# Loads of the next tile's input and of the last weight moved from ScalarE's DMA queue to GpSimd's, behind three small copies

## The chip, the cores and the metric

One core of one Trainium2 chip runs the whole kernel. The metric is the device time of one execution in microseconds; lower is better. Every run shown had the full TensorE clock granted.

## The reference, cut to what matters

One layer, 2048 tokens of width 1024, everything in float32. All weights below are inputs.

```
h = rms_norm(x) * g                                   # per token
u = h @ w_in   -> conv v, B, C, gate z | q, k, v, gate z | merge gate logits (2 x 1024)
y_a = (B * conv3(C * v) * silu(z)) @ w_conv_out        # causal depthwise, width 3
y_b = (window_attention(q, k, v, sinks) * silu(z_a)) @ w_attn_out   # window 128, 16 heads, 4 kv heads
g_a, g_b = sigmoid(gate logits + gate_b)
out = x + (g_a * y_a + g_b * y_b) @ w_out
```

## The kernel before

The 2048 tokens are two tiles of 1024. For each tile the program goes through the same stages: k, v and q projections, the four conv projections, the gates, the gated branches `za` and `z`, then `ya` (conv output projection) and at the end `yb` (attention output projection, which also adds the two gated branches). After both tiles the output projection `o` multiplies all tokens by `w_out`. Attention is woven into the projections and is over before `ya`.

TensorE (PE) works in banks of 128 x 512 results. Each float32 product is three passes in a reduced format, since every operand is kept as a high part, rounded by ScalarE (ACT), and a low part, the rest, subtracted by VectorE (DVE). Most stages use a seven-product scheme for 2 x 2 blocks, whose operands are sums of quarter blocks of the input; DVE forms these sums. The `yb` stage has plain products: four units, each of four banks, each bank 24 matmuls in two halves of 12. Two banks in PSUM alternate, so PE can begin a bank only when DVE has read the bank two before it.

The order on each engine is fixed by hand. A counter `tick` counts half banks; `put(n, f)` lays a step `f` at tick `n`, and `run` records PE's work with the steps due. Each engine then runs its own list in order and waits, at the head of the list, for what an instruction needs. A DMA is an instruction in the list of the engine that issues it. Its landing is counted on one of eight counters, taken in turn; DMAs of SyncE (SP) and ACT share one set of eight, GpSimd (POOL) has another eight. An issue also waits until the last DMA on its counter has landed.

During `yb` of a tile this happens beside PE:

- SP loads, for each pair of banks, two gate tiles `thb` (from `gd`) and two partial results `m` (from `md`); DVE reads a bank into `thb` (line 213, SCALAR_TENSOR_TENSOR `thb<-thb,yb`), adds `m`, and SP stores the result to `mt`. Two `thb` pairs exist, so a pair is loaded when the pair two before it has been stored.
- In tile 0, `next_tile` prepares tile 1: ACT issues eight loads of `x` (512 KB each, by tokens, `ld`), squares them (`xsq`, line 526) into row sums, DVE turns the sums into roots with a chain of 12 small steps per pair of `x` blocks and a copy into `rt` (line 530), PE transposes the roots (`ptr`, line 536), ACT copies them to `rb` (line 538). Two such sets exist: blocks 0 to 3 and 4 to 7. ACT also issues 16 loads of the transposed input, `h` (256 KB each, `raw_load`, line 561), DVE multiplies each by `rb` and the gain (`norm_l`, `norm_r`), and the sums and splits `oph` follow.
- In tile 1, `wo_side` loads `w_out` in 16 pieces `wo` of 256 KB, issued by ACT (line 1271), and forms its sums and splits. There are no squares and no roots in it.

GpSimd has work in the attention (moves, masks, stores) and none in `ya` and `yb`.

Of the kernel before, what the change touches and what calls it, by code (L numbers as in the profile page):

```python
# [8 lines left out]
F32 = mybir.dt.float32  # L9
# [6 lines left out]
P = 128  # L16
D = 1024
KC = D // P
T = 1024
H = 512  # L20
# [41 lines left out]
def block_kernel(  # L62
# [12 lines left out]
    nc = tc.nc  # L75
    S = x.shape[1]
    NT = S // T
    x2, out2, xt2, w_in2 = x[0], out[0], xt, w_in
    w_co, w_ao, w_o = w_conv_out, w_attn_out, w_out[0]
# [7 lines left out]
    small = ctx.enter_context(tc.tile_pool(name="small", bufs=12))  # L87
# [6 lines left out]
    def slot(shape, dt, name):  # L94
        return big.tile(shape, dt, tag="big", name=name)

    def optile(name, shape=(P, 2, H), dt=F32R):
        return oppool.tile(list(shape), dt, tag="op", name=name)
# [25 lines left out]
    def hs(q):  # L124
        return slice(q * H, (q + 1) * H)
# [117 lines left out]
    def add(o, a, b, eng=None):  # L243
        return (eng or vec).tensor_tensor(out=o, in0=a, in1=b, op=ALU.add)

    def sub(o, a, b, eng=None):
        return (eng or vec).tensor_tensor(out=o, in0=a, in1=b, op=ALU.subtract)
# [172 lines left out]
    def spare(name):  # L420
        return consts.tile([P, H], F32, tag="s5", bufs=2, name=name)
# [96 lines left out]
    def x_load(t, b, eng):  # L518
        xt = optile(f"x{t}_{b}", (P, D), F32)
        r0 = t * T + b * P  # L520
        eng.dma_start(xt, x2[r0 : r0 + P, :])
        return xt

    def x_square(xt, ss, i, junk=None):

        nc.scalar.activation(out=xt if junk is None else junk, in_=xt, func=AF.Square, accum_out=ss[:, i : i + 1])
# [31 lines left out]

    def raw_load(t, q, c, st):
        h = st["raw"][c, q] = slot([P, H], F32, f"h{t}_{q}_{c}")  # L560
        nc.scalar.dma_start(h, xt2[c * P : (c + 1) * P, t * T + q * H : t * T + (q + 1) * H])

    def norm_l(t, c, st):
        x_norm(st["raw"][c, 0], c, st["rb"][0])
# [6 lines left out]
    def norm_r(t, c, st):  # L571

        x_norm(st["raw"][c, 1], c, st["rb"][1])
# [11 lines left out]
    def last_sum(j, st, to=None):  # L585

        raw = st["raw"]
        o = st.setdefault("t4", {})[j] = raw[2 * j, 0] if to is None else to
        sub(o, raw[2 * j + 1, 0], raw[2 * j, 0])

    def form(t, m, j, st):
        raw = st["raw"]
        src = {8: (0, 1), 1: (0, 0), 2: (1, 0), 3: (1, 1), 5: (0, 0), 6: (0, 0), 7: (0, 1)}.get(m)
        op_split(t, m, j, raw[2 * j + src[0], src[1]] if src else st["t4"][j], st["ops"])
# [5 lines left out]
    def put(n, f):  # L600
        at.setdefault(max(n, tick[0] + 1), []).append(f)
# [537 lines left out]
    def split_op(src, name):  # L1139
        o = optile(name)  # L1140
        split(o[:, 0], o[:, 1], src)
        return o


    YB_CHUNKS = (0, 2, 4, 6, 1, 3, 5, 7)

# [16 lines left out]
    def quarters(order):  # L1163
        return [(hf, q) for q in order for hf in range(2)]

    def branch(t, key, j, opt, fin, order):
        u = unit((key, t, j))
        for n, (hf, q) in enumerate(quarters(order)):
            ps = bank(f"{key}{t}_{j}_{hf}_{q}")
            yield from mm_t(ps, u, hf, opt, q, n == 3)  # L1170
            fin(2 * j + hf, q, ps)
            yield
# [50 lines left out]
    def yb_unit(t, j, opt, order):  # L1223
        th, m1 = {}, {}

        def get(n):
            pair = upool.tile([P, 2 * H + 2], F32, tag="u", name=f"thb{t}_{j}_{n}")
            for i, (hf, q) in enumerate(quarters(order)[2 * n : 2 * n + 2]):
                k = 2 * j + hf
                th[k, q] = pair[:, hs(i)]  # L1230
                nc.sync.dma_start(th[k, q], gd[t][1][k, :, hs(q)])
                m1[k, q] = spare(f"m1{t}_{k}_{q}")
                nc.sync.dma_start(m1[k, q], md[t][k, :, hs(q)])

        def fin(k, q, ps):
            m = th[k, q]
            vec.scalar_tensor_tensor(
                out=m, in0=m, scalar=1.0, in1=ps, op0=ALU.add, op1=ALU.mult)
            add(m, m, m1[k, q])
            nc.sync.dma_start(mt[t][k, :, hs(q)], m)  # L1240

        return branch(t, "yb", j, opt, fin, order), get
# [22 lines left out]
    def wo_side(n0, st):  # L1265
        raw = st["raw"]

        def ld(c):
            for q in range(2):
                h = raw[c, q] = slot([P, H], F32, f"wo_{c}_{q}")  # L1270
                nc.scalar.dma_start(h, w_o[c * P : (c + 1) * P, hs(q)])

        def sums(j):
            a, b = 2 * j, 2 * j + 1
            sub(raw[a, 1], raw[b, 1], raw[a, 1])
            sub(raw[a, 0], raw[b, 1], raw[a, 0])

        for j in range(KP):
            for i in range(2):
                put(n0 + 2 * j + i, lambda c=2 * j + i: ld(c))  # L1280
            put(n0 + 6 + 2 * j, lambda j=j: form(2, 1, j, st))
            put(n0 + 7 + 2 * j, lambda j=j: sub(raw[2 * j, 0], raw[2 * j, 1], raw[2 * j, 0]))
            put(n0 + 8 + 2 * j, lambda j=j: form(2, 5, j, st))
            put(n0 + 9 + 2 * j, lambda j=j: sums(j))
            put(n0 + 17 + j, lambda j=j: form(2, 6, j, st))
            put(n0 + 28 + j, lambda j=j: form(2, 2, j, st))
            put(n0 + 30 + j, lambda j=j: form(2, 7, j, st))
            put(n0 + 22 + j, lambda j=j: last_sum(j, st))
            put(n0 + 32 + j // 2, lambda j=j: form(2, 3, j, st))
            put(n0 + 34 + j // 2, lambda j=j: form(2, 4, j, st))  # L1290
# [33 lines left out]
    for n in range(S // P // 2):  # L1324
        t, c0 = divmod(2 * n * P, T)
# [5 lines left out]
    def x_state(t):  # L1331
        return state.setdefault(t, {"raw": {}, "ops": {}, "x": {}, "ss": {}})
# [3 lines left out]
    st = x_state(0)  # L1336
    raw, ops, xs = st["raw"], st["ops"], st["x"]
# [26 lines left out]
    for n in range(KC // 2):  # L1364
        u, h = divmod(n, 2)
# [178 lines left out]
    def next_tile(t, n0):  # L1544

        st = x_state(t)
        raw, ops, xs = st["raw"], st["ops"], st["x"]

        def ld(b):
            xs[b] = x_load(t, b, nc.scalar)  # L1550

        def stats(b0):
            ss = st["ss"][b0] = small.tile([P, 2], F32, tag="sx", bufs=4, name=f"ss{t}_{b0}")
            junk = ps_s.tile([P, D], F32, tag="s", name=f"xsq{t}_{b0}")
            for i in range(2):
                x_square(xs[b0 + i], ss, i, junk)

        def norm(b0):
            q, i = divmod(b0, HB)
            if i == 0:  # L1560
                rt[q] = small.tile([P, HB], F32, tag="sr", bufs=2, name=f"rt{t}_{q}")
            seen_[b0] = x_rsqrt(t, b0, 2, st["ss"][b0], rt[q][:, i : i + 2])

        def roots(q):
            for b0 in (q * HB, q * HB + 2):
                seen_[b0]()
            st.setdefault("rb", {})[q] = x_roots(t, q, rt[q])

        rt, seen_ = {}, {}
        for b, n in enumerate((0, 1, 1, 2, 3, 4, 5, 6)):  # L1570
            put(n0 + n, lambda b=b: ld(b))
        for g, n in enumerate((4, 4, 8, 9)):
            put(n0 + n, lambda g=g: stats(2 * g))
        for g, n in enumerate((5, 6, 10, 11)):
            put(n0 + n, lambda g=g: norm(2 * g))
            put(n0 + n + 1, lambda g=g: seen_[2 * g]())
        for q, n in enumerate((8, 15)):
            put(n0 + n, lambda q=q: roots(q))
        for c in range(KC):
            put(n0 + 6 + c // 2, lambda c=c: raw_load(t, 0, c, st))  # L1580
            put(n0 + 8 + c // 2, lambda c=c: norm_l(t, c, st))
            put(n0 + (13 if c % 2 == 0 else 18) + c // 2, lambda c=c: raw_load(t, 1, c, st))
        for j in range(KP):
            put(n0 + 15 + j, lambda j=j: form(t, 1, j, st))
            put(n0 + 15 + j, lambda j=j: norm_r(t, 2 * j, st))
            put(n0 + 16 + j, lambda j=j: first_sum(j, st))
            put(n0 + 18 + j, lambda j=j: form(t, 5, j, st))
            put(n0 + 20 + j, lambda j=j: norm_r(t, 2 * j + 1, st))
            put(n0 + 21 + j, lambda j=j: third(2 * j + 1, st))
            put(n0 + 21 + j, lambda j=j: second_sum(j, st))  # L1590
            put(n0 + 24 + j, lambda j=j: form(t, 6, j, st))
            put(n0 + 28 + j, lambda j=j: form(t, 2, j, st))
            put(n0 + 30 + j, lambda j=j: form(t, 7, j, st))
            put(n0 + 25 + j, lambda j=j: last_sum(j, st))
            put(n0 + 32 + j // 2, lambda j=j: form(t, 3, j, st))
            put(n0 + 34 + j // 2, lambda j=j: form(t, 4, j, st))

    tick0 = 0
    for t in range(NT):
# [57 lines left out]
        n0 = tick[0]  # L1657
# [78 lines left out]
```

## Time and profile before

| | us |
|---|---|
| median of 3 runs | 1933.35 (1933.23 to 1933.41) |
| profiled execution, device time | 1935.05 |
| its span in the trace | 1933.3 |
| PE busy | 1914.6 (99%) |
| DVE busy | 1531.3 (79%) |
| ACT busy | 970.6 (50%) |
| POOL busy | 561.2 (29%) |

The trace counts its times from the start of the span. A timeline row gives start, duration, engine, line, operation and tiles (written `<-` read); in square brackets stands how long the engine was idle before it and what ended that. Engine names with a q (ACTq, SPq) are the queue of an engine: DMA issues stand there and are not counted as busy. Line 213 is a helper through which nearly all DVE work goes, line 240 the one of ACT's rounding copies; these are told apart by their tiles. `yb` of tile 0 lies at 808 to 900 us, `yb` of tile 1 at 1690 to 1777 us. The queues in the DMA part of the profile: q1 is SP's, q10 ACT's, q0 GpSimd's.

### The profile page before, as it was taken

Reading aid. Unit: us, or ns where it says so; the run is one execution under the profiler, and the core shown is the slowest. Engines: PE = TensorE matmul, PEld = TensorE weight load, DVE = VectorE, ACT = ScalarE, POOL = GpSimd, SP = SyncE. Lnnn points to the kernel's source line nnn. Section 1 sums busy time; section 2 is a strip of 40 time slices with the busy share of each in tenths; the row PEclk is TensorE's granted clock in tenths of the full one; section 3 lists DMA queues with packets and bytes.
Section 4 is the critical chain, followed back from the end, with each engine's and each line's share of the span. In section 5 each row is a group of like instructions: output and inputs, shape, how many; then the busy total and the mean of one; then the engine's idle time right before and its main releaser. Section 6 shows DMA issues by size and latency. Waiting matters only on the chain.

```text
span 1933.3 us, 27463 instructions
## 1 busy us (share of the span) xinstructions
PE 1914.6 (99%) x8774; PEld 1587.9 (82%) x8774; DVE 1531.3 (79%) x2612; ACT 970.6 (50%) x1932; POOL 561.2 (29%) x786
## 2 busy tenths in 40 slices
PE   9999999999999999999999999999999999999999
PEld 7778888888888888878878888888888888888887
DVE  7989899888886669679689788888998568766654
ACT  7655455556674344434555545556666335423221
POOL 2371443455663000000462433445554000000000
PEclk9999999999999999999999999999999999999999
DMA  8485454577776423884585554567776523776453
GB/s 305 104 218 170 152 169 158 179 219 233 230 239 214 149 102 131 299 295 156 149 222 144 171 158 140 167 210 247 235 239 210 194 99 125 254 262 191 157 173 111
DMA packets 219424, 366.55 MB, mean 190 GB/s; under 512 B 29264, under 2 KB 104016, under 8 KB 219280
## 3 DMA queue, kind: packets, MB, share of 16 engines
q1 hardware_dynamic: 189696, 288.96, 46.5%
q0 software_dynamic: 23680, 63.21, 12.0%
q10 hardware_dynamic: 5904, 12.62, 2.0%
q8 instruction: 70, 1.15, 0.2%
q14 instruction: 74, 0.61, 0.1%
HBM read 251.17 MB, written 113.51 MB: 189 GB/s over the span
## 4 chain that ended last, share of the span: by engine, by line
PE 84%; DVE 8%; DMA 4%; issue 2%; ACT 1%; POOL 1%; SPq 0%; DVEq 0%; ACTq 0%; POOLq 0%
PE Y L412 31%; PE yb L1155 5%; PE Vcv L412 5%; PE Xcv L412 4%; PE Xgb L412 2%; PE Vgb L412 2%; PE Xza L412 2%; PE Vza L412 2%; PE Vga L412 2%; PE Vo L412 2%; PE Xo L412 2%; PE Vz L412 2%; PE Xz L412 2%; PE po L1017 2%; PE Xga L412 2%; PE Vb L412 2%
## 5 line engine op out<-in xcount | busy, mean ns | idle before, releaser
L979 POOL DMA_DIRECT2D x<-fd x256 | 140.4, 554 | 87.9 <-DMA fd<-f 49.9
L1000 POOL TENSOR_SCALAR_AFFINE_SELECT xh<-xh 64x512 fp32r<-64x512 f32 x64 | 73.5, 1148 | 142.3 <-DVE xl L213 120.6
L952 ACT ACTIVATE p<-s,st,rq 128x128 f32<-128x128 f32 x256 | 113.2, 450 | 0.3 <-DMA od<-o 0.3
L972 POOL DMA_DIRECT2D fd<-f x64 | 36.8, 575 | 248.7 <-DVE f L213 217.0
L856 POOL DMA_DIRECT2D vd<-v x16 | 9.9, 624 | 335.3 <-DVE k_r L236 328.9
L1155 PE MATMUL yb<-opb,wyb_0h 128*128 128x512 f32 x256 | 79.3, 391 | 2.4 <-DVE thb L213 2.4
L412 PE MATMUL Xcv<-oph,wcv_ah 128*128 128x512 f32 x256 | 79.5, 392 | 0.0
L1155 PE MATMUL yb<-opb,wyb_1h 128*128 128x512 f32 x256 | 78.9, 389 | 0.0
L1000 POOL TENSOR_SCALAR_AFFINE_SELECT xl<-xl 64x512 fp32r<-64x512 f32 x64 | 69.3, 1083 | 4.4
L1155 PEld LDWEIGHTS yb<-opb,wyb_0h 128*128 128x128 f32 x256 | 47.6, 188 | 13.8 <-DVE thb L213 3.6
L1000 POOL TENSOR_SCALAR_AFFINE_SELECT yp<-yp 64x512 fp32r<-64x512 f32 x64 | 56.4, 882 | 4.2
L308 ACT CAST wcv_sh<-wcv_raw 128x1024 fp32r<-128x1024 f32 x16 | 16.9, 1057 | 79.1 <-DVE wcv_raw L213 79.1
L1155 PEld LDWEIGHTS yb<-opb,wyb_1h 128*128 128x128 f32 x256 | 48.0, 188 | 10.0
L213 DVE TENSOR_TENSOR o<-po,o 64x256 f32<-64x256 f32 x128 | 53.5, 418 | 2.7 <-ACT o L1029 1.6
L1000 POOL TENSOR_SCALAR_AFFINE_SELECT yp<-xl 64x512 fp32r<-64x512 f32 x64 | 54.5, 852 | 3.1
L412 PEld LDWEIGHTS Xcv<-oph,wcv_ah 128*128 128x128 f32 x256 | 47.3, 188 | 9.5
L774 POOL DMA_DIRECT2D q2d<-q_h x64 | 44.3, 692 | 26.7 <-ACT q_h L769 21.5
L213 DVE TENSOR_TENSOR ophc<-zin,ophc 128x512 fp32r<-128x512 f32 x64 | 42.4, 688 | 10.8 <-ACT ophc L240 10.8
L213 DVE SCALAR_TENSOR_TENSOR y<-u,cols,y 128x512 f32<-128x512 f32 x64 | 49.2, 770 | 2.0 <-ACT y L1066 0.8
L952 ACT ACTIVATION_READ_ACCUMULATOR p<-s,st,rq 128x1 f32 x256 | 50.9, 199 | 0.0
L213 DVE TENSOR_TENSOR p<-p,st 128x512 f32<-128x512 f32 x64 | 48.1, 752 | 2.9
L240 ACT CAST ophc<-zin 128x512 fp32r<-128x512 f32 x64 | 37.3, 621 | 26.0 <-DVE zin L213 26.0
(629 smaller groups left out, 6398.7 us busy)
## 6 DMA issues: line engine op xcount, KB each, us to landing
wcv_raw<-in_w_in SPq DMA_DIRECT2D x32, 512.0 KB, 4.2
q<-q2d SPq DMA_DIRECT2D x64, 256.0 KB, 4.3
fd<-f POOLq DMA_DIRECT2D x64, 256.0 KB, 3.7
v<-vd SPq DMA_DIRECT2D x128, 128.0 KB, 3.2
x<-fd POOLq DMA_DIRECT2D x256, 64.0 KB, 3.1
gd<-th SPq DMA_DIRECT2D x64, 256.0 KB, 3.0
wq_raw<-in_w_in SPq DMA_DIRECT2D x16, 512.0 KB, 5.1
q2d<-q_h POOLq DMA_DIRECT2D x64, 128.0 KB, 4.5
```

What stands on the lines that cost most here:

```text
L213: r = f(*args, **kw)
L240: nc.scalar.copy(hi, src)
L308: return (lambda: nc.scalar.copy(hi, src), lambda: vec.tensor_tensor(out=lo, in0=src, in1=hi.bitcast(F32), op=ALU.subtract))
L412: nc.tensor.matmul(ps, lhsT=w[:, j, :], rhs=b[:, m, :], start=start and j == 0 and i == 0, stop=j == KP - 1 and i == 2, skip_group_check=n ...
L774: nc.gpsimd.dma_start(q2d[t][j][half, q * 2 * HB : (q + 1) * 2 * HB, i, e, :], src[HALVES[e]].bitcast(F32).rearrange("p (b x) -> p b x", x ...
L856: nc.gpsimd.dma_start(to, v[half].bitcast(F32).rearrange("p b l d -> p b (l d)"))
L952: nc.scalar.activation(out=p[:, i, :], in_=sg[:, i, HD : 3 * HD], func=AF.Exp, bias=st[:, 1, i : i + 1], scale=rv[:, i // 2, i % 2 : i % 2 ...
L972: nc.gpsimd.dma_start(fd, f)
L979: nc.gpsimd.dma_start(x[QUADS[k]], src[k])
L1000: nc.gpsimd.affine_select(out=d4, in_=s4, pattern=[[0, 2], [-32 * sg, 2], [0, G], [-sg, 32]], compare_op=ALU.is_gt if prev else ALU.is_ge, ...
L1017: nc.tensor.matmul(po[:, cs], lhsT=v2[:, kind, :], rhs=xx[:, :, h * HD : (h + 1) * HD], start=n == 0, stop=n == 2)
L1155: nc.tensor.matmul(ps, lhsT=w[:, j, cs], rhs=o[:, m, :], start=n == 0 and i == 0, stop=n == KC - 1 and i == 2)
```

## The change

All loads of `x` and `h` of tile 1 and all loads of `w_out` are issued by GpSimd. GpSimd's list gets small copies (128 x 1) that read a value which something else has to write first, and since the list runs in order, the loads behind a copy are issued after it: `hold_g` reads the first `thb` tile of the stage, in both tiles; `hold_l` and `hold_r` read the first column of the two root tiles `rt`. The eight `h` loads of the left half are laid one tick later than before. The values that are computed do not change.

```diff
     def raw_load(t, q, c, st):
         h = st["raw"][c, q] = slot([P, H], F32, f"h{t}_{q}_{c}")
-        nc.scalar.dma_start(h, xt2[...])
+        nc.gpsimd.dma_start(h, xt2[...])
...
+    def hold(src, name):
+
+        nc.gpsimd.tensor_copy(small.tile([P, 1], F32, tag="hold", bufs=2, name=f"hold_{name}"), src)
...
     def yb_unit(t, j, opt, order):
...
                 nc.sync.dma_start(m1[k, q], md[t][k, :, hs(q)])
+            if j == n == 0:
+
+                hold(pair[:, 0:1], f"g{t}")
...
     def wo_side(n0, st):
...
-                nc.scalar.dma_start(h, w_o[c * P : (c + 1) * P, hs(q)])
+                nc.gpsimd.dma_start(h, w_o[c * P : (c + 1) * P, hs(q)])
...
     def next_tile(t, n0):
...
-            xs[b] = x_load(t, b, nc.scalar)
+            xs[b] = x_load(t, b, nc.gpsimd)
...
+        put(n0 + 7, lambda: hold(rt[0][:, 0:1], "l"))
+        put(n0 + 13, lambda: hold(rt[1][:, 0:1], "r"))
         for c in range(KC):
-            put(n0 + 6 + c // 2, lambda c=c: raw_load(t, 0, c, st))
+            put(n0 + 7 + c // 2, lambda c=c: raw_load(t, 0, c, st))
```

On ACT, in `yb` of tile 0, the rows from the last split of the attention output on, before the change (`x_1` is the second `x` block; the first load stands a little ahead; `xsq` squares, `wyb` is a weight piece rounded for PE):

```order
L521 DMA x_1_8105<-in_x 128x1024
L521 DMA x_2_8108<-in_x 128x1024
L521 DMA x_3_8127<-in_x 128x1024
L521 DMA x_4_8144<-in_x 128x1024
L521 DMA x_5_8166<-in_x 128x1024
L526 ACTIVATE xsq_0_8169,ss_0_8168<-x_0_8079 128x1024
L526 ACTIVATE xsq_0_8169,ss_0_8168<-x_1_8105 128x1024
L526 ACTIVATE xsq_2_8173,ss_2_8172<-x_2_8108 128x1024
L526 ACTIVATE xsq_2_8173,ss_2_8172<-x_3_8127 128x1024
L521 DMA x_6_8191<-in_x 128x1024
L521 DMA x_7_8214<-in_x 128x1024
L561 DMA h_0_0_8228<-in_xt 128x512
```

The same place on ACT in the changed kernel:

```order
L526 ACTIVATE xsq_0_8171,ss_0_8170<-x_0_8081 128x1024
L526 ACTIVATE xsq_0_8171,ss_0_8170<-x_1_8107 128x1024
L526 ACTIVATE xsq_2_8175,ss_2_8174<-x_2_8110 128x1024
L526 ACTIVATE xsq_2_8175,ss_2_8174<-x_3_8129 128x1024
L308 CAST wyb_2_0h<-wyb_2_raw_7992 128x1024
L526 ACTIVATE xsq_4_8281,ss_4_8280<-x_4_8146 128x1024
L526 ACTIVATE xsq_4_8281,ss_4_8280<-x_5_8168 128x1024
L538 COPY rb_0_8289<-ptr_0_8284 128x512
L308 CAST wyb_2_1h<-wyb_2_raw_7994 128x1024
```

The loads are gone from ACT's list; squares, weight roundings and the copy of the roots follow each other as before.

On GpSimd, between the last mask of tile 0's attention and the first store of tile 1's values, where nothing stood before, the changed kernel has (`h_0_0` is the left half of the first block of `h`):

```order
L1146 COPY hold_g_8049<-thb_0_0_8042 128x1
L521 DMA x_0_8081<-in_x 128x1024
L521 DMA x_1_8107<-in_x 128x1024
L521 DMA x_2_8110<-in_x 128x1024
L521 DMA x_3_8129<-in_x 128x1024
L521 DMA x_4_8146<-in_x 128x1024
L521 DMA x_5_8168<-in_x 128x1024
L521 DMA x_6_8193<-in_x 128x1024
L521 DMA x_7_8216<-in_x 128x1024
L1146 COPY hold_l<-rt_0_8195 128x1
L561 DMA h_0_0_8260<-in_xt 128x512
L561 DMA h_0_1_8262<-in_xt 128x512
```

All eight `x` loads stand directly behind `hold_g`, the left `h` loads behind `hold_l`; the right ones follow behind `hold_r`. Each hold waits for one write: `hold_g` for the first `thb` load, `hold_l` and `hold_r` for the copy of the first two columns of their `rt`, not for the second such copy. In tile 1, all 16 loads of `wo` stand behind the second `hold_g`. The lists of PE, DVE and SP keep their order.

More of the change, by code (lines that the diff above doesn't have):

```diff
@@ L560, in raw_load @@
         h = st["raw"][c, q] = slot([P, H], F32, f"h{t}_{q}_{c}")
-        nc.scalar.dma_start(h, xt2[c * P : (c + 1) * P, t * T + q * H : t * T + (q + 1) * H])
+        nc.gpsimd.dma_start(h, xt2[c * P : (c + 1) * P, t * T + q * H : t * T + (q + 1) * H])
     def norm_l(t, c, st):
```

## The prediction

> **What bounds the kernel now.** I read the page's busy times first, then the stretches of each stage, then PE's own waits in time order, and from them back to DVE and ACT.
>
> ```profile
> PE 1914.6 (99%) x8774; PEld 1587.9 (82%) x8774; DVE 1531.3 (79%) x2612; ACT 970.6 (50%) x1932; POOL 561.2 (29%) x786
> ```
>
> PE is busy for all but 1933.3 - 1914.6 = 18.7 us. The change adds and removes nothing on PE, so it can gain only where PE stands idle. The view of stretches shows how much that is around the change (span, then PE busy as the first number behind it; the last three columns are granted clock, DMA share, GB/s):
>
> ```profile
> 808.00:907.00 99.00, 96.57 (x426) 78.38 (x425) 79.19 (x159) 31.30 (x51) 0.00 (x0) 1.00 0.76 256
> 907.00:1000.00 93.00, 92.98 (x432) 76.20 (x431) 71.54 (x127) 51.86 (x89) 44.02 (x68) 1.00 0.62 170
> 1680.00:1778.00 98.00, 98.00 (x434) 81.16 (x433) 66.68 (x98) 26.96 (x41) 0.00 (x0) 1.00 0.74 238
> 815.00:820.00 5.00, 5.00 (x24) 4.14 (x23) 2.60 (x5) 0.42 (x1) 0.00 (x0) 1.00 0.86 298
> ```
>
> In `yb` of tile 0 PE idles 99.00 - 96.57 = 2.43 us; after it and in `yb` of tile 1 it idles for nothing. PE's timeline gives the places:
>
> ```profile
> 833.00 0.83 PE L536 MATMUL ptr<-ident,rt 128*128 128x128 f32 x4
> 842.54 0.73 PE L1155 MATMUL yb<-opb,wyb_0h 128*128 128x512 f32 x2 [0.51 <-DVE thb L213]
> 849.23 0.73 PE L1155 MATMUL yb<-opb,wyb_0h 128*128 128x512 f32 x2 [0.96 <-DVE thb L213]
> 855.75 0.70 PE L1155 MATMUL yb<-opb,wyb_0h 128*128 128x512 f32 x2 [0.29 <-DVE thb L213]
> 894.80 0.73 PE L1155 MATMUL yb<-opb,wyb_0h 128*128 128x512 f32 x2 [0.65 <-DVE thb L213]
> 900.40 0.62 PE L412 MATMUL Xk<-oph,wk_ah 128*128 128x512 f32 x2
> ```
>
> Four waits, 0.51 + 0.96 + 0.29 + 0.65 = 2.41 us, each for DVE to read a bank. The pair of matmuls behind a wait takes 0.70 to 0.73 instead of 0.62, so each costs 0.1 more. The ceiling of a gain is thus 2.41 + 0.4 = 2.8 us. That is 0.15%; 0.2% (3.87 us) is about what a measurement of this kernel can tell from no change.
>
> DVE in the same time shows why it is late:
>
> ```profile
> 817.36 0.69 DVE L213 SCALAR_TENSOR_TENSOR thb<-thb,yb 128x512 f32<-128x512 f32 x1 [4.41 <-DMA thb<-gd]
> 829.21 0.17 DVE L530 COPY rt<-hr_r 128x2 f32<-128x2 f32 x1
> 829.28 0.16 DVE L227 TENSOR_SCALAR ms<-ss 128x2 f32<-128x2 f32 x1
> 839.34 0.75 DVE L213 SCALAR_TENSOR_TENSOR h<-h,cols,rb 128x512 f32<-128x512 f32 x1 [6.00 <-ACT rb L538]
> 841.81 0.68 DVE L213 SCALAR_TENSOR_TENSOR thb<-thb,yb 128x512 f32<-128x512 f32 x1
> 846.07 0.75 DVE L213 SCALAR_TENSOR_TENSOR h<-h,cols,rb 128x512 f32<-128x512 f32 x1 [0.39 <-DMA h<-in_xt]
> 848.50 0.68 DVE L213 SCALAR_TENSOR_TENSOR thb<-thb,yb 128x512 f32<-128x512 f32 x1
> 850.79 0.17 DVE L530 COPY rt<-hr_r 128x2 f32<-128x2 f32 x1
> 851.24 0.75 DVE L213 SCALAR_TENSOR_TENSOR h<-h,cols,rb 128x512 f32<-128x512 f32 x1 [0.28 <-DMA h<-in_xt]
> 854.91 0.69 DVE L213 SCALAR_TENSOR_TENSOR thb<-thb,yb 128x512 f32<-128x512 f32 x1
> 858.17 0.74 DVE L213 SCALAR_TENSOR_TENSOR h<-h,cols,rb 128x512 f32<-128x512 f32 x1
> 862.92 0.69 DVE L213 SCALAR_TENSOR_TENSOR thb<-thb,yb 128x512 f32<-128x512 f32 x1 [0.88 <-DMA thb<-gd]
> 865.29 0.69 DVE L213 TENSOR_TENSOR thb<-thb,m 128x512 f32<-128x512 f32 x1 [1.67 <-DMA m<-md]
> 894.07 0.68 DVE L213 SCALAR_TENSOR_TENSOR thb<-thb,yb 128x512 f32<-128x512 f32 x1
> ```
>
> It stands idle 6.00 us for `rb`, and then reads its banks (841.81, 848.50, 854.91, 894.07) just too late. PE had finished the transposed roots at 833.00 + 0.83 = 833.8. ACT copied them only at 838.74, and its list shows why:
>
> ```profile
> 807.69 11.85 ACTq L521 DMA_DIRECT2D x<-in_x  x5
> 819.58 1.03 ACT L526 ACTIVATE xsq<-x 128x1024 f32<-128x1024 f32 x1 [11.48 <-DMA m<-md]
> ...
> 830.97 4.48 ACTq L561 DMA_DIRECT2D h<-in_xt  x4
> 835.54 1.06 ACT L308 CAST wyb_0h<-wyb_raw 128x1024 fp32r<-128x1024 f32 x1 [11.25 <-DMA h<-in_xt]
> ...
> 838.74 0.57 ACT L538 COPY rb<-ptr 128x512 f32<-128x512 f32 x1
> ```
>
> Twice, for 11.48 and 11.25 us, ACT stands behind load issues that wait for their counters; a weight rounding, two squares and `rb` queue behind the second block.
>
> **Prices.** From the views of single lines and tiles, in this order: ACT's `h` loads, GpSimd's `kd` stores (issue, then landing), GpSimd's small loads, the `x` loads, the `thb` loads and stores; then SP's issue of the first `thb`, and GpSimd's nearest small copy:
>
> ```profile
> DMA to landing us min/median/max: 3.6/4.5/6.8
> ...
> L695 POOL DMA_DIRECT2D kd<-k_h x16: 594/596/606, 87.6 to 978.5; - x16
> ...
> DMA to landing us min/median/max: 4.4/5.9/8.8
> ...
> L979 POOL DMA_DIRECT2D x<-fd x256: 551/551/581, 176.9 to 1477.5; - x128
> ...
> DMA to landing us min/median/max: 4.5/6.8/8.7
> ...
> DMA to landing us min/median/max: 2.0/5.3/8.7
> ...
> 809.86 0.40 SPq L1231 DMA_DIRECT2D thb<-gd  x1
> ...
> L148 POOL CAST mask_i<-mask_f 64x64 int32<-64x64 f32 x2 | 0.5, 233 | 0.1
> ```
>
> **The change part by part.** *ACT's list* loses 40 issues and both blocks. The time itself is off the path; it counts only through `rb`.
>
> *hold_g.* The first `thb` was issued at 809.86 and let DVE go at 817.36, 7.5 us later, with `x` loads beside it. Without them it lands after 2.0 to 7.5 us; I take the median 5.3, so 815.2. The copy adds up to 0.23, each issue 0.6: blocks 0 to 3 are issued by 815.4 + 4 x 0.6 = 817.8 and land 6.8 later, at 824.6 (4.5 to 8.7: 822.3 to 826.5). The last square and its sum take 1.2 us, so 825.8. DVE's second root chain needs them at 829.28: 3.5 us to spare. The other bound is the rate: 4 x 0.52 = 2.1 MB at half of the 298 GB/s, the other half going to SP's loads, take 14.1 us, so 815.4 + 14.1 + 1.2 = 830.7, which is 1.4 us late. Behind that chain stands `ptr` on PE, whose 0.83 us show that it hardly waited; each late us there is PE's. So 0 to +1.4; I take +0.4, nearer to the landings, which are of the same transfers.
>
> *rb.* It stands on ACT behind the squares of blocks 4 and 5. By landings these are in at 819.0 + 6.8 = 825.8, by half the rate (3.1 MB) at 836.5. Squared 2.4 us later, `rb` follows at 834 (straight after `ptr`) to 839 (no gain). I take 835.
>
> *hold_l* waits for the first copy into `rt`, done at 829.38. With 0.23 and 0.6 the first `h` load is issued at 830.2, and the next three within 1.8 us, where ACT needed 4.48 us from 830.97. It lands 4.5 (`h` on ACT) to 5.9 us (`kd` on GpSimd) later, 834.7 to 836.1. So DVE begins on `h` at about 835.5 instead of 839.34: 3.8 us earlier (0 to 5). For the first three waits to go it must be 0.51, 1.47 and 1.76 us earlier at 841.81, 848.50 and 854.91, and its own waits of 0.39 and 0.28 for `h` loads go too. All three go: -1.76.
>
> *hold_r* follows the copy of 850.79, now about 847.0; with 0.83 and 4.5 to 5.9 its first load is in at 852.3 to 853.7, needed at 858.17 - 3.8 = 854.4. No cost, by 0.7 us at the worse end.
>
> *The last wait.* From 855 to 905 DVE hardly rests but for 0.88 and 1.67 us, for `thb` and `m`. To clear 894.80 it has to be 1.76 + 0.65 = 2.4 us earlier there. Its adds and SP's stores come 2 to 3 us earlier, and so do the loads that wait for these stores; GpSimd's eight right `h` loads, now in a row, run against them. I take 0.45 of the 0.65.
>
> *Restarts:* 3.5 of the four at 0.1: -0.35.
>
> *Tile 1.* PE has no wait to lose. The 16 `wo` loads (4.2 MB) now start together after the first `thb`. The nearest place:
>
> ```profile
> 1711.67 0.69 DVE L213 SCALAR_TENSOR_TENSOR thb<-thb,yb 128x512 f32<-128x512 f32 x1 [3.42 <-PE yb L1155]
> 1719.50 0.69 DVE L213 SCALAR_TENSOR_TENSOR thb<-thb,yb 128x512 f32<-128x512 f32 x1 [2.69 <-DMA thb<-gd]
> ```
>
> A bank takes 87 us / 16 = 5.4; the one complete before 1711.67 is followed by one complete at 1717.1, whose place PE needs at 1722.5. DVE ends its read at 1720.2: 2.3 us to spare. From median to longest landing is 3.4 us, so 0 to +1.1; I take 0.
>
> **Sum:** -1.76 - 0.45 - 0.35 + 0.4 = -2.16. The profiled execution took 1935.05, 1.75 above its span and 1.70 above the median, so it would become 1932.9; the median 1933.35 becomes **1931.2** us. With the ceiling, and with both unknown costs: 1930.5 to 1933.7.
>
> **Rivals.** *The gain is given back.* If the `thb` and `m` loads of 862.92 and 865.29 land no earlier, DVE's lead ends there, PE arrives 1.76 us sooner at 894.80 and waits that much longer. Likewise if `rb` follows at 839. For it: SP's loads wait for stores that share the transfers with GpSimd's eight. Against: the stores are issued earlier. Then 1933.35, give or take 0.5.
>
> *The x loads come late.* All eight start only after `hold_g`, where two went out before 809 on ACT. If they got a third of 298 GB/s, blocks 0 to 3 would need 21 us: 815.4 + 21 + 1.2 = 837.6, 8.3 us too late, all of it PE's at `ptr`. It decides from a landing of block 3 at about 828. Half the rate gives +1.4; the middle is +5, so 1938. For it: DMA engines 86% busy at 815 to 820. Against: landings of 8.7 at most.
>
> *GpSimd is held at its issues by DVE.* If an issue waited for three DVE operations of 0.75 us, it would take 2.85; block 3 would be issued at 826.8, squared at 834.8, 5.5 us late: with the other gains lost, 1938.9. Against: 256 issues beside a DVE that is 79% busy lie between 551 and 581 ns. [...]
>
> **How the numbers follow.** Forecast 0.55; given back 0.23; late `x` loads 0.13; held issues 0.05; a gain beyond the ceiling 0.04. Of the late loads and the held issues, 0.09 lie above 1937.2, and 0.03 more for mishaps in tile 1: slower 0.12, faster 0.04, same 0.84. The range 1930.3 to 1936.0 holds the forecast, the given-back case and the milder third of the others: about 0.83. Gains and losses within 0.2% share most of it.
>
> **What would show it.** Right: `rb` before 836; DVE's idle time before its first `h` below 3 us; no PE wait at the banks near 842, 849 and 856; PE idle below 1 us in the stretch 808 to 907. Wrong: `ptr` with a wait of over 1 us on PE, `xsq` of block 3 after 829, GpSimd issues over 0.7 us, a PE wait in `yb` of tile 1, or a longer wait near 893.

## The result, and the profile after

The changed kernel took 1938.05 us in the median of 9 runs (1937.52 to 1939.37), the kernel before 1933.95 in 9 runs beside it. The ratio is 1.0023, with a 95% interval of 1.0012 to 1.0033: slower by 4.1 us, where a gain of 2.2 was forecast. The profiled execution of the changed kernel took 1939.21 us, its span is 1937.5.

The page's busy times:

```profile
PE 1915.4 (99%) x8774; PEld 1588.2 (82%) x8774; DVE 1530.6 (79%) x2612; ACT 967.7 (50%) x1932; POOL 582.6 (30%) x830
```

PE does the same work; it now stands idle for 1937.5 - 1915.4 = 22.1 us instead of 18.7. The view of stretches tells where (span, PE, PEld, DVE, ACT, POOL busy; clock, DMA share, GB/s):

```profile
808.00:907.00 99.00, 94.64 (x414) 76.38 (x413) 76.77 (x156) 29.27 (x48) 13.72 (x27) 1.00 0.73 255
907.00:1000.00 93.00, 93.00 (x433) 76.57 (x433) 72.27 (x128) 52.58 (x90) 42.66 (x67) 1.00 0.62 172
1680.00:1778.00 98.00, 96.01 (x423) 78.86 (x422) 65.00 (x96) 26.37 (x41) 8.82 (x17) 1.00 0.74 244
815.00:820.00 5.00, 5.00 (x23) 4.13 (x22) 4.19 (x6) 0.00 (x0) 4.44 (x9) 1.00 0.89 317
```

In `yb` of tile 0 PE idles 99.00 - 94.64 = 4.36 us instead of 2.43, in `yb` of tile 1 for 1.99 instead of nothing. That is 3.92 us of the 4.2 by which the span grew. PE's timeline has the single waits:

```profile
832.93 0.83 PE L536 MATMUL ptr<-ident,rt 128*128 128x128 f32 x4
843.02 0.73 PE L1159 MATMUL yb<-opb,wyb_0h 128*128 128x512 f32 x2 [1.08 <-DVE thb L213]
849.08 0.73 PE L1159 MATMUL yb<-opb,wyb_0h 128*128 128x512 f32 x2 [0.32 <-DVE thb L213]
867.66 0.74 PE L1159 MATMUL yb<-opb,wyb_0h 128*128 128x512 f32 x2 [1.24 <-DVE thb L213]
874.49 0.72 PE L1159 MATMUL yb<-opb,wyb_0h 128*128 128x512 f32 x2 [1.05 <-DVE thb L213]
897.18 0.73 PE L1159 MATMUL yb<-opb,wyb_0h 128*128 128x512 f32 x2 [0.63 <-DVE thb L213]
...
1724.49 0.72 PE L1159 MATMUL yb<-opb,wyb_0h 128*128 128x512 f32 x2 [0.41 <-DVE thb L213]
1731.82 0.73 PE L1159 MATMUL yb<-opb,wyb_0h 128*128 128x512 f32 x2 [1.58 <-DVE thb L213]
```

The waits near 842 and 849 are still there, two new ones stand at 867 and 874, and two in tile 1. All are for DVE's read of a bank, as before. What DVE waited for is in its timeline:

```profile
815.23 0.69 DVE L213 SCALAR_TENSOR_TENSOR thb<-thb,yb 128x512 f32<-128x512 f32 x1 [2.34 <-POOL hold_g L1146]
824.97 0.69 DVE L213 SCALAR_TENSOR_TENSOR thb<-thb,yb 128x512 f32<-128x512 f32 x1 [4.03 <-PE yb L1159]
836.19 0.75 DVE L213 SCALAR_TENSOR_TENSOR h<-h,cols,rb 128x512 f32<-128x512 f32 x1 [2.92 <-DMA h<-in_xt]
842.28 0.69 DVE L213 SCALAR_TENSOR_TENSOR thb<-thb,yb 128x512 f32<-128x512 f32 x1 [3.55 <-DMA thb<-gd]
858.94 0.75 DVE L213 SCALAR_TENSOR_TENSOR h<-h,cols,rb 128x512 f32<-128x512 f32 x1 [1.15 <-DMA h<-in_xt]
866.92 0.69 DVE L213 SCALAR_TENSOR_TENSOR thb<-thb,yb 128x512 f32<-128x512 f32 x1 [4.10 <-DMA thb<-gd]
...
1723.74 0.69 DVE L213 SCALAR_TENSOR_TENSOR thb<-thb,yb 128x512 f32<-128x512 f32 x1 [5.37 <-DMA thb<-gd]
```

DVE does begin on `h` at 836.19, 3.15 us earlier than before. But then it waits for `thb` loads of SP: 3.55 us at 842.28, where it did not wait before, and 4.10 at 866.92, where it was 0.88. GpSimd's timeline shows what is in flight by then:

```profile
815.01 0.18 POOL L1146 COPY hold_g<-thb 128x1 f32<-128x1 f32 x1 [207.18 <-DMA thb<-gd]
815.60 4.26 POOL L521 DMA_DIRECT2D x<-in_x  x8 [0.41 <-issue]
829.48 3.29 POOL L561 DMA_DIRECT2D h<-in_xt  x6 [0.40 <-issue]
...
851.55 1.07 POOL L561 DMA_DIRECT2D h<-in_xt  x2
853.21 3.21 POOL L561 DMA_DIRECT2D h<-in_xt  x6 [0.59 <-DMA m<-md]
```

And SP's own queue, with its stores of results and the `thb` loads that wait for them, first before, then in the changed kernel:

```profile
822.84 0.50 SPq L1240 DMA_DIRECT2D mt<-thb  x1
827.86 0.33 SPq L1240 DMA_DIRECT2D mt<-thb  x1
834.60 0.33 SPq L1231 DMA_DIRECT2D thb<-gd  x1
```

```profile
821.34 0.58 SPq L1247 DMA_DIRECT2D mt<-thb  x1
822.94 0.44 SPq L1247 DMA_DIRECT2D mt<-thb  x1
836.61 0.33 SPq L1235 DMA_DIRECT2D thb<-gd  x1
...
850.15 0.42 SPq L1247 DMA_DIRECT2D mt<-thb  x1
851.63 0.51 SPq L1247 DMA_DIRECT2D mt<-thb  x1
861.45 0.33 SPq L1235 DMA_DIRECT2D thb<-gd  x1
```

A `thb` pair is loaded into the place of the pair two before it, so its load waits for both `mt` stores of that pair. The stores of 821.34 and 822.94 were issued earlier than before, and the load behind them came later: 836.61 instead of 834.60. The store of 822.94 took 13.6 us to land, that is until 836.5; before, the one of 827.86 took 6.7, until 834.6. The view of the `mt` tile in the stretch 808 to 907 has the longest landing, first of before (that of 822.84), then of after:

```profile
DMA to landing us min/median/max: 2.0/4.8/8.1
```

```profile
DMA to landing us min/median/max: 2.4/5.0/13.6
```

The view of stretches for 821 to 837 has the engines' load, before and after (last columns: DMA share, GB/s):

```profile
821.00:837.00 16.00, 15.98 (x73) 13.04 (x72) 8.02 (x33) 4.68 (x8) 0.00 (x0) 1.00 0.89 327
```

```profile
821.00:837.00 16.00, 15.98 (x73) 13.04 (x72) 7.41 (x32) 10.14 (x18) 4.46 (x9) 1.00 1.02 403
```

In the changed kernel the 16 DMA engines are full from end to end of it (share 1.02), at 403 GB/s.

DVE's read at 866.92 is 4.0 us later than before, and half of that is the `thb` load's own. The store of 851.63 took 9.8 us (before, that of 851.75 took 7.8), and the `thb` load behind it landed 5.3 us after its issue instead of 3.2.

**Theory.** GpSimd's DMAs count on eight counters apart from the eight of SP and ACT (556 and 1265 DMAs in this trace; none was issued before the last on its counter had landed). With nothing between its issues, it starts 2 to 4 MB in a few us (a burst: eight `x` loads of 512 KB in the 4.26 us from 815.60, eight right `h` loads of 256 KB in the 4.87 from 851.55). The engines fill up, SP's `mt` stores land late, the `thb` loads behind them are issued late and may land late themselves, DVE reads its banks late, PE waits. **Rivals.** (1) The queue: transfers that GpSimd issues delay SP's, or arrive late, at any pace. (2) Write after read: DVE overwrites the first `thb` in place, and now waits for `hold_g` to have read it; that lateness is carried through the stage.

### The profile page after: what moved, and what is told of

Read it like the earlier page. It is cut to its first block, busy times and chain, and to the rows that moved or that the text cites. A ratio compares the mean times of both kernels' runs of the same rounds, so it can differ in the third digit from the quotient of the medians.

```text
span 1937.5 us, 27524 instructions
## 1 busy us (share of the span) xinstructions
PE 1915.4 (99%) x8774; PEld 1588.2 (82%) x8774; DVE 1530.6 (79%) x2612; ACT 967.7 (50%) x1932; POOL 582.6 (30%) x830
## 3 DMA queue, kind: packets, MB, share of 16 engines
q0 software_dynamic: 27392, 75.80, 13.6%
## 4 chain that ended last, share of the span: by engine, by line
PE 81%; DVE 8%; DMA 6%; issue 2%; ACT 1%; POOL 1%; SPq 0%; DVEq 0%; POOLq 0%; ACTq 0%
PE Y L412 31%; PE Vcv L412 5%; PE Xcv L412 4%; PE yb L1159 3%; PE Xgb L412 2%; PE Vgb L412 2%; PE Xza L412 2%; PE Vza L412 2%; PE Vga L412 2%; PE Vo L412 2%; PE Xo L412 2%; PE Vz L412 2%; PE Xz L412 2%; PE po L1017 2%; PE Xga L412 2%; DMA mt<-thb 2%
## 5 line engine op out<-in xcount | busy, mean ns | idle before, releaser
L213 DVE SCALAR_TENSOR_TENSOR thb<-thb,yb 128x512 f32<-128x512 f32 x32 | 21.9, 684 | 43.9 <-PE yb L1159 24.1
```

The costliest lines, as they stand in the source:

```text
L213: r = f(*args, **kw)
```

## The experiments

PE's idle time is read from the stretches 808 to 907 and 1680 to 1778 of each profiled run. The ratio is against the kernel before, beside it on the same chip, with its 95% interval; it is the measured ratio of the runs and not always the quotient of the two medians. Two kernels ran only once. Each idle time is that of a single execution, and one kernel can differ much between two: e6 and e12 are the same kernel.

| kernel | PE idle, `yb` tile 0 | PE idle, `yb` tile 1 | median us | ratio |
|---|---|---|---|---|
| before | 2.43 | 0.00 | 1933.95 | 1 |
| changed | 4.36 | 1.99 | 1938.05 | 1.0023 [1.0012, 1.0033] |
| e1: next tile only | 3.85 | 0.00 | 1936.9 | 1.0014 [1.0005, 1.0023] |
| e2: `wo` only | 2.66 | 1.10 | 1935.62 | 1.0007 [0.9998, 1.0016] |
| e3: no `hold_g` | 5.59 | 0.81 | 1939.23 | 1.0028 [1.0017, 1.0040] |
| e4: `wo` spread | 4.27 | 0.00 | 1936.8 | 1.0009 [1.0000, 1.0018] |
| e5: e4, `x` on ACT | 3.83 | 0.00 | 1935.8 | 1.0009 [1.0000, 1.0017] |
| e6: e5, `h` spread | 0.05 | 0.00 | 1932.76 | 0.9991 [0.9982, 1.0000] |
| e7: e4, `h` spread | 1.23 | 0.00 | 1933.98 | 1.0001 [0.9992, 1.0010] |
| e8: e7, two `x` first | 2.05 | 0.00 | 1933.58 | 0.9996 [0.9988, 1.0005] |
| e9: e6, right `h` in a row | 3.33 | 0.00 | 1936.37 | one run |
| e10: e6, `wo` on ACT | 0.02 | 0.00 | 1932.21 | 0.9993 [0.9984, 1.0002] |
| e11: before, with extra copies | 2.90 | 8.16 | 1946.71 | one run |
| e12: e6 again | 2.04 | 0.00 | 1932.31 | 0.9990 [0.9981, 0.9999] |

**Which tile loses (e1, e2).** One part of the change alone:

```diff
-                nc.gpsimd.dma_start(h, w_o[c * P : (c + 1) * P, hs(q)])     # e1
+                nc.scalar.dma_start(h, w_o[c * P : (c + 1) * P, hs(q)])
...
-            xs[b] = x_load(t, b, nc.gpsimd)                                 # e2, and h likewise
+            xs[b] = x_load(t, b, nc.scalar)
```

> Only the loads of the next tile stand on GpSimd (with hold_g, hold_l and hold_r); the w_out loads stand on ACT's queue as before. Theory (a burst of loads fills the DMA engines, SP's stores of mt land some 14 us after their issue, the thb loads that wait for them are late, DVE is late, PE waits): the two tiles lose separately, so this keeps tile 0's loss (PE idle in yb of tile 0 about 4.4 us against 2.43) and loses nothing in yb of tile 1 (idle below 0.2): +1.9 to +2.2 us over before, about 2 us under the changed kernel. Rival (one common cause, such as DVE's first overwriting of thb waiting for the copies, or GpSimd's queue being slow as such): also 2 us less here, so this run alone only sizes the two parts; if the loss stays at +4, the parts are not separate.

> Only the w_out loads stand on GpSimd, behind hold_g of tile 1; x and h loads stand on ACT at their places of before. Theory: yb of tile 0 as before (PE idle 2.4 us), yb of tile 1 idle 2.0 us with a thb load issued some 4 us later than before: +2.0 us over before. With e1 the two differences should add up to that of the changed kernel (+4.1).

The code shows only the lines that moved back. e1 also has `hold_g` in tile 0 only; e2 has it in tile 1 only, without `hold_l` and `hold_r` and with the left `h` loads at their old tick.

The parts are separate: e1 has idle time above before's in tile 0 alone, e2 nearly all of its own in tile 1, and 0.0014 + 0.0007 come close to 0.0023. In size both missed: e1's median is 2.8 us over that of before (1934.12 in the runs beside it) for 1.42 us more idle time, e2's 1.5 instead of 2.0. A possible reason for e1's surplus stands in the last section.

**The holds (e3).** Without the two `hold_g`:

```diff
-            if j == n == 0:
-                hold(pair[:, 0:1], f"g{t}")
```

> The changed kernel without its two hold_g copies: GpSimd issues x and w_out loads as soon as their buffers are free. Theory (burst): the bursts come some us earlier, not weaker. The first thb loads of tile 0 and 1 land later (by up to 4 us), the mt stores of about 821 and 1705 then find emptier engines and land within 8 us instead of 14; PE's idle time in yb of tile 0 falls from 4.4 to 2 to 3 us and in tile 1 from 2.0 to 0 to 1: 1 to 4 us under the changed kernel, unless the first thb is so late that it makes a new wait. Rival (DVE's first overwriting of thb waits for the copy, 3.42 us in the trace, and that lateness is what PE pays): both tiles' losses go, whatever the mt stores do. The mt landings tell them apart: if the stores still take 14 us and the waits are gone, the rival holds.

In tile 1 PE idles 0.81 instead of 1.99, all of it at a new place, 1706. In tile 0 the condition after "unless" came true; PE's timeline:

```profile
823.55 1.19 PE L1159 MATMUL yb<-opb,wyb_0h 128*128 128x512 f32 x2 [4.34 <-DVE thb L213]
```

The first `thb` and `m` loads, issued from 813.04 on, now meet the `x` loads at full DMA engines (a share of 1.02 and 1.03 from 810 to 815 and 815 to 820); DVE stands idle for 10.11 us before it begins on its first bank at 822.72, by its row until an `m` load landed, and PE waits for 4.34 us. The sign that the expectation named is the landing of the stores. Both stores of the first pair in tile 0, issued at 828.19 and 829.67, when the `x` burst was over, took 3.8 and 7.9 us instead of 8.4 and 13.6. In tile 1 the expected burst did not form: without the hold the `wo` loads went out two or three at a time from 1683 to 1698, and the slowest store took 8.0 instead of 14.3. The waits near 843 and 849 and those of 1724 and 1731 are gone with them, as the theory has it; the total says nothing here, since the new wait outweighs them.

Against rival (2) speaks the changed kernel itself: with `hold_g` DVE reads its first bank at 815.23, earlier than before (817.36), and then stands idle for 4.03 us until PE's bank at 824.97, so no lateness of the hold is carried on. Rival (2) falls as the main cause.

**The pace, on the same queue (e4).** Four more small copies in tile 1, of the first four results of `thb`, let the 16 `wo` loads out in groups:

```diff
             nc.sync.dma_start(mt[t][k, :, hs(q)], m)
+            if t == 1 and j == 0:
+                hold(m[:, 0:1], f"t{t}_{k}_{q}")
```

> The changed kernel with four more small copies on GpSimd in tile 1, one of each of the first four results of thb, so that the 16 w_out loads go out in groups of 2, 4, 4, 4, 2, one group for each bank, on the same queue. Theory (burst): rate of about 200 GB/s instead of all at once, mt stores land within 9 us, no PE wait in yb of tile 1: about 2 us under the changed kernel (-1.6 to -2.2). Rival (the queue itself, its descriptors or its share of the engines, delays SP's transfers whenever it is used): same bytes on the same queue in the same stage, so at least half of the 2.0 us stays. Rival (write after read on thb behind the copies): more copies, so no less than 2.0 us.

The view of stretches, tile 1:

```profile
1680.00:1778.00 98.00, 98.00 (x434) 81.12 (x433) 67.14 (x99) 28.59 (x44) 10.51 (x21) 1.00 0.76 251
```

PE's 1.99 us are gone with the same bytes on the same queue, so rival (1) cannot carry the loss of tile 1. All seven profiled runs with this spread (e4 to e9 and e12) idle for 0.00 there, the two with the `wo` loads in a row (changed and e2) for 1.99 and 1.10. One expectation missed: the slowest `mt` store there still took 12.5 us (14.3 in the changed kernel). It was enough: the `thb` load behind it came 27.3 us after the start of `yb` (1720.02 after 1692.73), with the burst 29.6 (1720.87 after 1691.28), and before 27.1 (1716.77 after 1689.71).

**The three bursts of tile 0 (e5 to e9).** e5 puts the `x` loads back on ACT at their old places. e6 also spreads the `h` loads:

```diff
-        put(n0 + 13, lambda: hold(rt[1][:, 0:1], "r"))
...
+        def spread_l(c):      # called ahead of raw_load(t, 0, c, st)
+            src = {2: lambda: st["rb"][0], 4: lambda: raw[0, 0], 6: lambda: raw[1, 0]}.get(c)
+            if src:
+                hold(src()[:, 0:1], f"l{c}")
+        def spread_r(c):      # called ahead of raw_load(t, 1, c, st)
+            if c == 1:
+                hold(raw[0, 1][:, 0:1], "r1")
```

e7 has the `h` loads spread and the `x` loads in a row as in the changed kernel, e8 two of them ahead of `hold_g`; e9 is e6 with `hold_r` again and `spread_r` empty. All have e4's spread in tile 1.

> As the run with the spread w_out loads, and in tile 0 the x loads stand on ACT's queue at their places of before (no hold_g there); only the h loads are on GpSimd, behind hold_l and hold_r. Theory (burst): the first thb pair waits for mt stores that no longer share the engines with eight x loads in a row, so it is issued at about 834 to 835 as before (836.6 to 837.8 with the burst), and DVE's wait for thb near 842 goes from 3.6 us to under 1. ACT's list has lost its h issues, so rb still comes at 834 to 836. The eight right h loads in a row stay, so the wait for thb near 866 (2.9 to 4.1 us) stays. PE idle in yb of tile 0: 1.5 to 3 us; total 0 to +1 us against before. Rival (it is the h loads, not the x loads, that hold the mt stores of 821): the thb pair still at 836 to 838 and idle of 4 us: +2.

> As the run before it, and the h loads are spread: the left ones in pairs behind rb and behind the first and second normalised h, the right ones for even rows without hold_r, those for odd rows behind the first normalised right h. Theory (burst): both thb waits go (near 842 under 0.5 us, near 866 under 1.5), rb at 834 to 836, PE idle in yb of tile 0 at 0.3 to 1.3 us: 1 to 2 us under before (the only kernel here with a gain). Rival (GpSimd's transfers as such delay SP's): same bytes on the same queue, idle stays at 3 us or more.

> As the run with the spread w_out loads, x loads in a row on GpSimd behind hold_g as in the changed kernel, h loads spread. Theory (burst): the eight x loads in a row alone are 4 MB at 815 to 829 and hold the mt stores of 821 and 823, so the thb pair comes at 834 to 837 and DVE still waits 1 to 3 us near 842; the wait near 866 goes to under 1.5 us. PE idle 1.5 to 3: 0 to +1 against before. If the left h loads were the cause, thb comes before 834 and the idle falls below 1.

> As the run before it, with hold_g moved behind the first two x loads, so that only six x loads (3 MB) start together at 815. Theory (burst): the first thb lands 1 to 2.5 us later (816 to 818), the mt stores of 821 to 824 land 2 to 3 us earlier, the thb pair is issued at 832 to 835: PE idle 0.5 to 2 us in tile 0, -1.5 to 0 against before. Rival (any early x load costs more at the first thb than it brings at the second): a PE wait before 832, as with no hold_g at all (4.34 us near 823).

> As the run that spread x (by ACT's own list), h and w_out, but the right h loads stand again in a row of eight behind hold_r, as in the changed kernel; the left ones stay spread. Theory (burst): the two ends of the stage come apart. Near 842 all stays clear (thb pair issued at 833 to 835, no wait over 0.5 us), while the mt stores of about 848 to 850 meet the eight right loads: the thb pair behind them is issued at 860 to 862 instead of 856.6, DVE waits 2 to 4 us for it near 863 to 866, and PE idles 0.5 to 2.5 us at 860 to 880. Rival (only the left loads mattered, and their lateness is carried along): PE idle stays below 0.3 us.

The stretch 808 to 907 of e6:

```profile
808.00:907.00 99.00, 98.95 (x439) 81.33 (x438) 82.83 (x164) 34.27 (x55) 10.33 (x21) 1.00 0.76 261
```

No PE wait is left: the whole idle time of before is gone too. PE's timeline of e9, with the right `h` loads in a row again, has everything clear up to 866, and then:

```profile
867.03 0.74 PE L1159 MATMUL yb<-opb,wyb_0h 128*128 128x512 f32 x2 [1.57 <-DVE thb L213]
873.83 0.74 PE L1159 MATMUL yb<-opb,wyb_0h 128*128 128x512 f32 x2 [1.02 <-DVE thb L213]
896.53 0.74 PE L1159 MATMUL yb<-opb,wyb_0h 128*128 128x512 f32 x2 [0.60 <-DVE thb L213]
```

SP's queue in e9, to be read against the same rows of the changed kernel:

```profile
849.12 0.42 SPq L1247 DMA_DIRECT2D mt<-thb  x1
...
850.60 0.51 SPq L1247 DMA_DIRECT2D mt<-thb  x1
860.78 0.33 SPq L1235 DMA_DIRECT2D thb<-gd  x1
```

In e6 the stores of 847.87 and 849.28 let the pair go at 856.64. In e9 the store of 850.60 took 10.2 us and the `thb` load behind it 5.3; in e6 the same two took 7.3 and 2.7, in e12 8.2 and 4.0. The waits at 867, 874 and 896 make 3.19 us, more than the 0.5 to 2.5 expected. Not all of that need be the row's: e12, in which the right loads are spread, has 1.29 + 0.60 us in the same stretch. So in these single executions the eight right loads in a row cost 1.3 to 3.2 us.

At the left end `x` and left `h` loads share the blame, against the expectation of e5 that it is the `x` loads. Counted from PE's first `yb` matmul, the third `thb` pair was issued after 26.1 us before (834.60 - 808.52), 28.2 in the changed kernel, 26.9 in e5 (only `h` in a row), 27.9 in e7 (only `x` in a row) and 25.5 in e6 (neither). The two act at different places. The `x` loads in a row hold the store ahead of the pair: the later store of the first pair took 13.6 us in the changed kernel and 13.4 in e7, but 7.8 in e5, 7.0 in e6 and 6.7 before. The left `h` loads in a row go with a slow landing of the `thb` load itself: 5.5 us in the changed kernel and 6.3 in e5, but 4.5 in e7 and 2.9 in e6. Before the change it was 5.5 too, with ACT's `h` loads beside it. In e5 DVE still waited 3.65 us for that pair, where under 1 was expected, but the wait ended at 842.57, in time for PE to lose only 0.55 and 0.31; its other waits, 0.72, 1.49 and 0.65 near 867, 875 and 897, are those of the right loads. With the median 1.8 us over before, e5 missed its bound of +1. e7 kept a wait of 2.36 us near 863 (expected: under 1.5) and idled less than expected, 1.23; against e6 and e12 that is no clear difference in idle time (0.05 and 2.04), and 1.2 to 1.7 us in the medians. e8 tells nothing of an earlier start: its copy stood in GpSimd's list behind the first bank's result and ended only at 817.8, so its six `x` loads started later than the eight of e7.

**Is a gain left, and whose (e10, e12)?** e10 is e6 with the `wo` loads back on ACT and no `hold_g`; e12 is e6 once more.

> Only the spread h loads stand on GpSimd; x and w_out loads stand on ACT as before, with no hold_g at all. Theory: yb of tile 1 idles for nothing on either queue, so this equals the run with everything spread: PE idle in yb of tile 0 at 0 to 1 us, 1 to 2.5 us under before. If the spread w_out loads on GpSimd had brought a gain of their own, this would be slower than that run.

> The kernel with x on ACT and h and w_out spread on GpSimd, once more, to narrow its ratio against before: 0.9988 to 0.9995 if the four waits of before are gone in most executions.

In `yb`, e10 equals e6 in its profile. e12 comes out at 0.9990 [0.9981, 0.9999], its profile with two waits (1.29 and 0.60) where e6's had none: the spread order clears the waits in some executions and not in all. It is faster than before by 0.1%, 1.8 us between the medians (before: 1934.06), at the edge of what these runs can tell. It is the lowest ratio here, not told apart from e6 and e10.

**Traffic alone (e11).** The kernel before, with 16 copies in tile 1 that nothing needs:

```diff
                 nc.scalar.dma_start(h, w_o[c * P : (c + 1) * P, hs(q)])
+                nc.gpsimd.dma_start(extra[c, q], w_o[c * P : (c + 1) * P, hs(q)])
```

Of the edit only the copies are shown; they stand behind a `hold_g` of tile 1 as in the changed kernel.

> The kernel before, with 16 additional copies of 256 KB each that nothing needs (w_out read again, written to an unused array in DRAM), issued by GpSimd in a row behind a copy of the first thb of tile 1. No load that the kernel uses is moved. Theory (the transfers of other queues hold the mt stores, not a later use of the data): yb of tile 1, without a wait before, now has mt stores of 1705 to 1709 that take 14 us or more, thb loads 4 us or more late, DVE waiting for thb, and a PE wait of 1 to 5 us. Rival (the loads moved to GpSimd arrive late themselves, and DVE and ACT are held by them): nothing waits, +0.0.

PE's timeline, and DVE's:

```profile
1732.08 1.22 PE L1160 MATMUL yb<-opb,wyb_0h 128*128 128x512 f32 x2 [8.16 <-DVE thb L213]
```

```profile
1725.21 1.29 DVE L213 TENSOR_TENSOR oph<-wo,oph 128x512 fp32r<-128x512 f32 x2 [10.12 <-ACT oph L240]
1731.34 0.69 DVE L213 SCALAR_TENSOR_TENSOR thb<-thb,yb 128x512 f32<-128x512 f32 x1 [3.70 <-DMA thb<-gd]
```

Traffic that no instruction waits for makes a PE wait of 8.16 us in a stage that had none. The sign is the theory's. The size is beyond the 1 to 5 us, and the path is not the expected one. The `wo` loads on ACT, not moved at all, came late too; the view of DMA issues for 1696 to 1724 (KB each, median us to landing), before and in e11:

```profile
wo<-in_w_out ACTq DMA_DIRECT2D x11, 256.0 KB, 5.7
```

```profile
wo<-in_w_out ACTq DMA_DIRECT2D x13, 256.0 KB, 10.5
```

The `mt` stores, expected at 14 us or more, took only up to 8.9 us to land but were issued late, at 1710.89 and 1719.49: SP's list stood 8.13 us at two weight loads between them (in e3 the issue of two takes 0.96, at 828.67), 7.3 of these waiting for a `wo` load of ACT, by the view of SP's waits. SP and ACT share their eight counters; before the change, too, this line of SP waited up to 2.6 us for a `wo` load that it does not read (the same view, 1690 to 1740). So here the late loads of one queue held the list of another. e11 thus shows that traffic on GpSimd's queue delayed the others, and not that it did so through the stores' landing.

## Why the prediction was wrong

- *Right:* everything up to DVE's first `h`. `hold_g` ended at 815.2 (forecast 815.2 for the landing), block 3 was squared at 827.4 (825.8; needed at 829.28), `ptr` did not wait (so the +0.4 taken for it was 0), and the first `h` load was issued at 829.5 (830.2). ACT copied `rb` when `ptr` was done, at 833.79 (835):

```profile
833.79 0.59 ACT L538 COPY rb<-ptr 128x512 f32<-128x512 f32 x1 [2.52 <-PE ptr L536]
```

- *The step that failed first: "All three go: -1.76".* It moved DVE's reads of the banks up with its `h` work and never asked for the arrival of what those reads also need: the `thb` pair whose load hangs on two `mt` stores. That pair came 2 us later, because the `x` loads, now in a row, held the store ahead of it (13.6 us to land; 7.0 and 7.8 in e6 and e5, which have them on ACT). Even before the change it had landed only at 834.60 + 5.5 = 840.1, 1.7 us ahead of DVE's read at 841.81, so a lead of 3.8 us could not reach that read without an earlier pair. Measured at these three places: 1.08 + 0.32 + 0 = 1.40 us instead of 0.
- *The last wait, -0.45.* The text saw that "GpSimd's eight right `h` loads run against them" and let the stores win. e9 shows the reverse: the eight alone cost 1.3 us against e12 and 3.2 against e6. Measured in the changed kernel: 1.24 + 1.05 + 0.63 instead of 0.20.
- *Tile 1, "0 to +1.1; I take 0".* Mis-sized: 1.99. The bound came from the longest landing seen before (3.4 us above the median); a burst has no such row to be bounded by. The slowest `mt` store there took 14.3 us instead of the 7.9 of before.
- *Restarts:* seven waits in both tiles instead of four, so +0.3 instead of -0.35.
- *The range.* Its upper end of "1930.5 to 1933.7" counts the +0.4 twice; the working gives 1933.3. The measured time lies far above both.
- *Rivals.* "The gain is given back" had the right place and mechanism, stores that share the transfers with GpSimd's eight, but let the `thb` load come no later than before. It came 4.0 us later at 866.92, and tile 1 lost besides. "The x loads come late" was wrong: block 3 was there at 826.27. "GpSimd is held at its issues by DVE" too: eight issues in 4.26 us, 0.53 each, from 815.6 on, while DVE was busy for 4.19 of the 5.00 us of the stretch 815 to 820.
- Not weighed: what transfers issued by one engine do to those of another. e11 measured it: with the copies on GpSimd's queue the median landing of ACT's loads went from 5.7 to 10.5 us. In the change, with the loads on another engine's queue, SP's slowest `mt` store of tile 0 went from 8.1 to 13.6 us, and the cost was 4.1 us.

Not settled: how much of the delay of one `mt` store is waiting behind other queues' packets and how much is slower packets of its own; no run separates them. Nor does any run say how often a spread order clears all waits: two profiled executions of that kernel idle for 0.05 and 2.04 us.

## What to carry to other kernels

Before moving loads to an idle queue, ask what paced them where they were: here it was ACT's in-order list and the completion counters shared with SP (before, ACT's `x` load of 819.17 went out when an `m` load of SP on its counter had landed, at 819.15), and taking that pace away let 2 to 4 MB start at once. Then list every store and load of the other queues in that window, and follow the one whose landing something on the critical path waits for, two steps back if a buffer is reused. If the move is wanted for its order, keep a pace on the new queue: small copies of values that appear at the rate at which the loads are needed, with the `x` loads back on ACT, turned +4.1 us into about -1.8 (e12). With the `x` loads left in a row on GpSimd the copies brought it to no difference (e7).

## What the runs showed of the hardware

**PE's clock halved after some waits of 1.88 us and more.** The granted clock of each whole run was 0.997 to 1.0, but there are stretches at half clock inside. e1 had a PE wait of 1.88 us and e4 one of 3.63. The stretches right behind them (PE's clock is the third number from the end):

```profile
845.00:849.00 4.00, 4.00 (x12) 3.13 (x11) 4.00 (x7) 0.00 (x0) 0.00 (x0) 0.57 0.22 73
```

```profile
844.00:852.00 8.00, 6.46 (x17) 5.06 (x18) 7.03 (x16) 0.00 (x0) 0.00 (x0) 0.57 0.41 134
```

PE's timeline of e4 shows what half a clock is for a pair of matmuls that otherwise takes 0.62 us:

```profile
845.54 1.22 PE L1159 MATMUL yb<-opb,wyb_0h 128*128 128x512 f32 x2 [3.63 <-DVE thb L213]
846.98 1.05 PE L1159 MATMUL yb<-opb,wyb_0h 128*128 128x512 f32 x2
```

0.43 of 4 us and 0.43 of 8 us lost at half clock make 3.4 and 6.9 us spent there. So the one wait cost up to 1.7 us more than its own length, the other up to 3.4; in the profiled executions e1 and e4 lost more than their idle time by this. Their medians are of other executions, whose waits no trace shows. No wait up to 1.8 us did this (that of e3 near 26 us). Of the waits of 1.9 to 2.5 us some did and some did not: the one near 26 us halved the clock in the profiled runs of e1 (1.91), e9 (2.01), e5 (2.04) and e10 (2.45), and not in before (2.09), e6 (2.13) or e11 (2.30). Part of the scatter of the times, 2 to 7 us within one of these kernels, may come from this, by the author's guess; no run took that wait away. Summed over the views of stretches, the half clock lasts 3.4 us after the waits of 1.88 to 2.45, and 6.8 to 6.9 after those of 3.63, 4.34 and 8.16. What makes one wait halve the clock and not another was not shown.

**A store's landing time depended on the traffic beside it.** The 256 KB `mt` stores took 2.0 to 8.1 us before and up to 13.6 beside a burst, at an unchanged median (4.8 and 5.0): the stage was set by the few slowest, which a median does not show.
